# Hybrid decoder trunk: the ends of both attentions and the norms behind them issued in another order and on other engines

## Chip, cores and metric

One core of one Trainium2 chip runs the whole program. The metric is the device time of one execution in microseconds (us), less is better. Before the change three runs gave a median of 1220.93 us (1218.38 to 1221.46).

The core has five engines that run side by side and wait for each other by semaphores: TensorE (PE in the profile; PEld is its weight load), VectorE (DVE), ScalarE (ACT), GpSimd (POOL) and SyncE (SP), which here issues nearly all DMAs.

## The reference

A trunk of two layers over 512 positions of 1024 values. Layer 0 mixes with two groups of attention heads (MoBA and NSA), layer 1 with forgetting attention (FoX); behind each mixer stands an MLP with squared ReLU, and a norm stands ahead of each of the four.

```python
def reference(x, rel_bias, mix_norm, mlp_norm, even_w_in, even_w_out, ...):
    h = x
    for layer in range(DEPTH):
        hn = rmsnorm(h, mix_norm[layer])
        i = layer // 2
        if layer % 2 == 0:
            h = h + moba_nsa_mixer(hn, even_w_in[i], even_w_out[i], rel_bias, ...)
        else:
            h = h + fox_mixer(hn, odd_w_in[i], odd_b_forget[i], odd_w_out[i])
        h = h + sqrelu_mlp(rmsnorm(h, mlp_norm[layer]), mlp_w1[layer], mlp_w2[layer])
    return rmsnorm(h, final_norm)
```

Both mixers end in `o @ w_out`, where `o` holds 16 heads of 64 columns. The kernel treats them as 8 pairs of heads, so `w_out` falls into 8 blocks of 128 rows, one for each pair. `sqrelu_mlp` is `relu(h @ w1)**2 @ w2` with 4096 inner columns.

## The kernel before

**Data.** The 512 positions are four tiles `x0` to `x3` of 128 x 1024 float32 in SBUF (in the rows of the trace all are `x`), the residual stream `h`. Each product in float32 is made of three passes: both factors are split into a high part (rounded, by ScalarE) and a low part (the rest, by a subtraction), and `mm3` (L136 to L138) multiplies high by high, high by low and low by high into one PSUM bank. Its matmuls write up to 128 x 512.

**Weights.** `split` (L94, L101) takes a loaded block of 128 x 1024 from the pool `raw` (5 buffers), lets ScalarE write the high part (L94) and VectorE or GpSimd the low part (L101) into a buffer of the pool `whl` (3 buffers). Which of the two makes the low part is read from a string of D and P (`MIX0_LOW`, `FOX_LOW`), letter by letter.

**Order.** Each mixer runs a list of steps, `MIX0_ORDER` and `FOX_ORDER`. In it `k`/`n`/`m` (layer 0) and `k`/`p` (layer 1) are logits, softmax and products with V for a pair of heads; `x` loads the first four blocks of `w1` and squares them on ScalarE (L429, each leaves a sum); `y` multiplies these sums on TensorE (L411), makes a power-of-two scale from them on VectorE (L416 to L419), and splits the four blocks by that scale into float16 parts (L438 on ScalarE, L439 on VectorE); `o67:01` is the output projection of the pairs 6 and 7 for the tiles 0 and 1. The framework's scheduler then orders each engine's instructions by priority; head work has a higher one (`prio`), so that independent matmuls fill in between. Behind that each engine works through its own queue in order.

**Output projection.** `out_proj` makes for each tile two groups of matmuls (3 for each pair of heads) in two PSUM banks named `acc`, and after each group VectorE adds the bank to the tile (L673, 128 x 512). The bank is free for the next group but one when that add is done. Before, layer 0 splits the last four pairs' products in groups of 1, 6 and 23, layer 1 in groups of 2 pairs.

**Softmax of layer 0.** Logits (L509) are read by VectorE with the bias and the row's minimum (L513), turned by ScalarE's exponential (L514), normalised by GpSimd (L516), transposed on TensorE (L531), copied to a high part by ScalarE (L533, `PTh`) and to a low part by VectorE (L534, `PTl`), and multiplied with V (L604). A pair's result is put together by ScalarE (L645) and VectorE (L646) and split by GpSimd (L498 high, L654 low) into `O`.

**Softmax of layer 1.** Logits (L548) of Q and K, which ScalarE copies from PSUM (L1461, L1464) and VectorE and GpSimd split (L492, L494, L498); VectorE L552, ScalarE L553; high and low parts `HL` by ScalarE (L563, L570), VectorE (L571) and GpSimd (L564); a DMA transposes them into `HT` (L573), and TensorE multiplies by V (L627).

**The norm ahead of the MLP.** `norm_t16`, for each tile: ScalarE squares the tile and sums it (L377); three small operations of VectorE make a power-of-two factor from the sum's bits (L380 to L382); VectorE multiplies tile, factor and gain in two halves (L384); TensorE transposes (L389, 8 for a tile); ScalarE and VectorE copy high and low parts out (L392, L393). The gain row `g` comes by a DMA (L158). The first MLP stage then multiplies float16 parts in matmuls of 128 x 256, first for the tiles 0 and 1, then for 2 and 3.

Of the kernel before, what the change touches and what calls it, by code (L numbers as in the profile page):

```python
# [49 lines left out]

class Trunk:
# [370 lines left out]
    def up_load(self, layer, s, pool, tag, tiles, squares, behind=None):  # L422
        w = self.I["mlp_w1"][layer]
        raws = [pool.tile([P, W_RAW], F32, tag=tag, name=self.nm("w1")) for _ in range(4)]
        for f, raw in enumerate(raws):
            c = 512 * s + P * f
            self.nc.sync.dma_start(raw.rearrange("p (k c) -> p k c", k=KD), w[:, c:c + P].rearrange("(k p) c -> p k c", p=P))
            with self.tc.issue_after(behind.ins) if behind else ExitStack():
                self.nc.scalar.activation(tiles[f][:, 1], raw, AF.Square, accum_out=squares[:, f:f + 1])  # L429
# [19 lines left out]
    def prepare_mlp(self, layer):  # L449
# [9 lines left out]
        def rest():
            self.scales16(st[:, 0], st[:, 1:], "s", self.pv_last)(self.v_last)  # L460
            self.first_up = self.up_split(raws, st[:, 1:], tiles), st[:, 1:]
        self.prepare_rest = rest
# [74 lines left out]
    def softmax_t(self, passes, band):  # L537
# [6 lines left out]
        for qi in (3, 2, 1, 0):  # L544
            w = P * (qi + 1)
            ps = self.psum("s" if qi % 2 else "pt")
            for i, (q, k) in enumerate(passes):
                nc.tensor.matmul(ps[:, :w], q[:, qi * P:(qi + 1) * P], k[:, :w],  # L548
# [108 lines left out]
    def out_proj(self, w, arg, os, hs, pools={}):  # L657
# [3 lines left out]
        if tiles[0] == 0:  # L661
            for i in pairs:
                self.wout[i] = self.rows(w, P * i, 1, pools.get(i))[0]
# [890 lines left out]
```

## Time and profile before

| | |
|---|---|
| median of three runs | 1220.93 us |
| the profiled execution | 1220.05 us |
| its span in the trace | 1218.0 us |
| mean granted TensorE clock | 0.993 |

The span is what the trace shows from the first to the last instruction; the 2.05 us around it are not in the trace. A row of the timeline has start, length, engine, line, operation, tile written and tiles read, shapes, and in brackets the idle time of the engine ahead of the row and what ended it. In a row of the windows each engine has its busy time in the stretch and in brackets its instructions, then come the granted clock (1.00 is full), the DMA engines' share and their GB/s. Matmuls overlap in their records: the step between the starts of two is what one costs.

### The profile page before, as it was taken

To read this page: it belongs to the slowest core of one execution; us is meant where nothing else is said; L and a number is where in the kernel's file an instruction comes from. 1 tells how busy PE (TensorE), PEld (TensorE's weight loads), DVE (VectorE), ACT (ScalarE), POOL (GpSimd) and SP (SyncE) were. 2 spreads that over 40 slices of the span, in tenths; PEclk is the share of its full clock that TensorE was granted. 3 is DMA by queue.
4 is the path that set the end of the run, shared out by engine and by line. 5 is a ranking of instruction groups with operands and counts; after the bars stand their busy time and mean duration, and the time that the engine had idled before them with its cause. 6 is when DMAs were issued, how large, how long until landed. Compare 5 with 4: busy or idle time off the path is not lost. (4 is left out here: it accounts for less than half of the span.)

```text
span 1218.0 us, 17306 instructions
## 1 busy us (share of the span) xinstructions
PE 1181.6 (97%) x6203; PEld 872.3 (72%) x6203; DVE 934.0 (77%) x1741; ACT 738.9 (61%) x1355; POOL 344.8 (28%) x391
## 2 busy tenths in 40 slices
PE   9999999998999999999998999999999999999997
PEld 7789987876855665666687878887675566656666
DVE  6877678888779687978767677676859787779865
ACT  7447656684686575656416785685478466746442
POOL 3434557451030322111001553443003032112104
PEclk9999999999999999999999999999999999999999
DMA  8962332114333244224005475545734413442201
GB/s 238 335 179 59 87 104 79 53 44 139 90 112 115 83 138 139 68 72 149 1 27 143 115 160 119 130 112 120 212 105 121 139 45 111 138 121 64 75 1 70
DMA packets 183729, 134.28 MB, mean 110 GB/s; under 512 B 48163, under 2 KB 158923, under 8 KB 183644
## 3 DMA queue, kind: packets, MB, share of 16 engines
q1 hardware_dynamic: 183484, 132.95, 38.8%
q8 instruction: 49, 0.80, 0.3%
q14 instruction: 36, 0.29, 0.1%
q10 hardware_dynamic: 160, 0.23, 0.1%
HBM read 120.28 MB, written 7.64 MB: 105 GB/s over the span
## 5 line engine op out<-in xcount | busy, mean ns | idle before, releaser
L136 PE MATMUL acc<-x,w 128*128 128x512 f16 (+1 forms) x512 | 187.6, 366 | 0.0
L138 PE MATMUL acc<-x,w 128*128 128x512 f16 (+1 forms) x512 | 187.4, 366 | 0.0
L137 PE MATMUL acc<-x,w 128*128 128x512 f16 (+1 forms) x512 | 187.3, 366 | 0.0
L1300 PE MATMUL s<-whl,sp 128*128 128x512 f32 x672 | 180.2, 408 | 0.1
L1300 PEld LDWEIGHTS s<-whl,sp 128*128 128x128 f32 x672 | 126.1, 188 | 32.5 <-DVE x L1309 1.4
L1253 DVE TENSOR_TENSOR whl<-w,whl 128x1024 fp32r<-128x1024 f32 x98 | 122.1, 1261 | 13.8 <-ACT whl L1252 13.8
L1252 ACT ACTIVATE whl<-w 128x1024 fp32r<-128x1024 f32 x98 | 99.8, 1048 | 53.4 <-DVE w L1258 34.4
L1309 DVE SCALAR_TENSOR_TENSOR x<-s,nr,x 128x512 f32<-128x512 f32 x112 | 82.2, 744 | 62.6 <-PE s L1300 62.6
L94 ACT ACTIVATE whl<-raw 128x1024 fp32r<-128x1024 f32 (+1 forms) x75 | 77.7, 1044 | 49.2 <-PE acc L138 20.2
L1219 POOL TENSOR_TENSOR t<-act 128x512 f32<-128x512 f32 x14 | 25.6, 1831 | 282.5 <-ACT act L1198 171.6
L136 PEld LDWEIGHTS <-w 128*128 128x128 f16 x576 | 57.1, 99 | 56.9 <-issue 10.9
L138 PEld LDWEIGHTS <-w 128*128 128x128 f16 x576 | 56.3, 98 | 56.2 <-issue 5.3
L1196 ACT ACTIVATE r<-acc,upsc 128x512 f32<-128x512 f32 x56 | 38.2, 682 | 96.1 <-PE acc L138 96.1
L136 PE MATMUL acc<-xhi,whl 128*128 128x512 f32 x240 | 94.9, 396 | 1.4 <-DVE Q L494 0.9
L138 PE MATMUL acc<-xhi,whl 128*128 128x512 f32 x240 | 94.6, 394 | 1.3 <-POOL whl L101 0.8
L137 PE MATMUL acc<-xlo,whl 128*128 128x512 f32 x240 | 93.9, 391 | 0.0
L137 PEld LDWEIGHTS <-w 128*128 128x128 f16 x576 | 56.5, 98 | 49.4 <-issue 2.4
L1300 PE MATMUL o<-whl,sp 128*128 128x512 f32 x336 | 83.5, 393 | 3.1 <-ACT sp L1208 3.1
L1258 DVE TENSOR_TENSOR w<-w,w 128x1024 f32<-128x1024 f32 x56 | 72.8, 1300 | 10.4 <-DMA w<-in_mlp_w 9.9
L101 DVE TENSOR_TENSOR whl<-raw,whl 128x1024 fp32r<-128x1024 f32 (+2 forms) x54 | 68.9, 1282 | 15.4 <-ACT whl L94 15.2
L439 DVE SCALAR_TENSOR_TENSOR w<-w,upsc,w 128x1024 f16<-128x1024 f32 x56 | 70.6, 1314 | 8.8 <-ACT w L438 8.8
L1300 PEld LDWEIGHTS o<-whl,sp 128*128 128x128 f32 x336 | 62.9, 188 | 17.4 <-ACT sp L1208 3.9
(339 smaller groups left out, 2923.4 us busy)
## 6 DMA issues: line engine op xcount, KB each, us to landing
w<-in_mlp_w SPq DMA_DIRECT2D x120, 512.0 KB
raw<-in_odd_w_in SPq DMA_DIRECT2D x22, 512.0 KB
raw<-in_even_w_in SPq DMA_DIRECT2D x20, 512.0 KB
band<-bias_dram SPq DMA_DIRECT2D x24, 256.0 KB
bias_dram<-bias_rows SPq DMA_DIRECT2D x16, 320.0 KB
raw<-in_even_w_out SPq DMA_DIRECT2D x8, 512.0 KB
raw<-in_mlp_w SPq DMA_DIRECT2D x8, 512.0 KB
raw<-in_odd_w_out SPq DMA_DIRECT2D x8, 512.0 KB
```

The source lines that it names most:

```text
L94: nc.scalar.activation(hl[:, 0, :n], raw[:, :n], AF.Copy)
L101: eng.tensor_tensor(hl[:, 1, :n], raw[:, :n], hl[:, 0, :n].bitcast(F32), op=ALU.subtract)
L136: mm(ps, ahl[0], bhl[0], start=first, stop=False)
L137: mm(ps, ahl[0], bhl[1], start=False, stop=False)
L138: self.mm_last = mm(ps, ahl[1], bhl[0], start=False, stop=last)
L439: nc.vector.scalar_tensor_tensor(t[:, 1], raw, y, t[:, 0], op0=ALU.mult, op1=ALU.subtract)
L1196: nc.scalar.activation(r, ps, AF.Relu, scale=undo[:, 1, f:f + 1])
L1252: nc.scalar.activation(t[:, 0], src, AF.Copy)
L1253: nc.vector.tensor_tensor(t[:, 1], src, t[:, 0].bitcast(F32), op=ALU.subtract)
L1258: nc.vector.tensor_tensor(out, a_, b_, op=op)
L1300: mm = lambda l, r, first, last: nc.tensor.matmul(ps, l, r, start=first, stop=last, skip_group_check=True)
L1309: self.added = nc.vector.scalar_tensor_tensor(hv, ps, by_token(t), hv, op0=ALU.mult, op1=ALU.add)
```

## The change

- **Order lists.** Layer 0: `x` moves ahead of the pair `m2`, `y` ahead of `m3`, the last pair. Before, the projection of the pairs 1 and 7 stood behind `m3` together with 6, 2 and 3; now 17 keeps its groups for the tiles 0 to 3, pair 6 alone remains for the tiles 2 and 3, and 6, 2, 3 go together for the tiles 0 and 1. So 12 adds follow in place of 16. A new step `z` splits the `w1` blocks two at a time. Layer 1: 45 runs for all four tiles ahead of 67.
- **Late output weights.** The rows for the pairs 2 and 3 (layer 0) and 5, 6, 7 (layer 1) are loaded into buffers of the softmax's pool `pP`, where the probabilities of done heads stood (`out_row`); their low part is made by the engine named there.
- **Squares.** In layer 0 they are issued behind the last product with V known then (`behind`); in layer 1 they are written to a buffer of its own, and not to the `w1` buffers.
- **Scale.** In layer 1 its matmul is issued behind the first of the last pair's logits.
- **Norm.** Tile times gain on GpSimd, the small factor on GpSimd in two operations, and the multiplication by it on ScalarE.

```diff
-MIX0_ORDER = "... n3 k3 m2 x0 m3 y o17:0123 o6:012 o23:01 o6:3 o23:23"
+MIX0_ORDER = "... n3 k3 x0 m2 y m3 o17:0123 o6:23 z01 o623:01 z23 o23:23"
-FOX_ORDER = "... o23:0123 x1 p7 y o45:012 o67:01 o45:3 o67:23"
+FOX_ORDER = "... o23:0123 x1 p7 y o45:0123 z01 o67:01 z23 o67:23"
...
-                nc.scalar.activation(xn[:, c], hs[t][:, c], AF.Square, accum_out=ssq[:, t + i:t + i + 1])
+                nc.scalar.activation(scratch[:, c], hs[t][:, c], AF.Square, accum_out=ssq[:, t + i:t + i + 1])
...
-            v.tensor_scalar(one(near).bitcast(I32), one(ssq).bitcast(I32), 1, None, op0=ALU.logical_shift_right)
-            v.tensor_scalar(one(near).bitcast(I32), one(near).bitcast(I32), -1, ROOT_BITS, op0=ALU.mult, op1=ALU.add)
-            v.tensor_tensor(one(scale), one(near), gain, op=ALU.mult)
-            for c in halves:
-                v.scalar_tensor_tensor(xn[:, c], hs[t][:, c], one(scale), g[:, c], op0=ALU.mult, op1=ALU.mult)
+            nc.gpsimd.tensor_tensor(xn, hs[t], g, op=ALU.mult)
+            nc.gpsimd.tensor_scalar(one(near).bitcast(I32), one(ssq).bitcast(I32), -0.5, ROOT_BITS, op0=ALU.mult, op1=ALU.add)
+            nc.gpsimd.tensor_tensor(one(scale), one(near), gain, op=ALU.mult)
+            nc.scalar.activation(xn, xn, AF.Copy, scale=one(scale))
...
+    def out_row(self, w, i, raw, parts, eng):
+        nc = self.nc
+        raw = raw.tile([P, PTW if raw is self.pP else W_RAW], F32, tag="P" if raw is self.pP else "raw", name=self.nm("raw"))
+        nc.sync.dma_start(raw[:, :D], w[P * i:P * i + P, :])
+        t = parts.tile([P, 2, W_RAW], FR, tag="whl", name=self.nm("whl"))
+        hl = t[:, 0], t[:, 1]
+        nc.scalar.activation(hl[0], raw[:, :D], AF.Copy)
+        eng.tensor_tensor(hl[1], raw[:, :D], hl[0].bitcast(F32), op=ALU.subtract)
+        return hl
...
+            how = {2: (self.pP, self.whl, nc.vector), 3: (self.pP, self.whl, nc.gpsimd)}
...
-                    self.prepare_mlp(int(arg))
+                    self.prepare_mlp(int(arg), self.pv_last)
...
-                    self.prepare_rest()
-                    self.phase = "D"
+                    self.prepare_rest(self.pv_last, self.v_last)
+                elif op == "z":
+                    for f in arg:
+                        self.prepare_part(int(f))
...
+            how = {5: (self.pP, last, nc.vector), 6: (self.pP, self.whl, nc.gpsimd), 7: (self.pP, self.whl, nc.gpsimd)}
...
-                    self.prepare_mlp(int(arg))
+                    self.prepare_mlp(int(arg), None, last.tile([P, 2, W_RAW], FR, tag="whl", name="dump2")[:, 0])
...
-                    self.prepare_rest()
-                    self.phase = "D"
+                    self.prepare_rest(self.logits_mid, self.v_mid)
```

In the rows below a name's number is its buffer, and each row is one instruction of the engine's queue in order. The first place is TensorE at the products with V of layer 0's last head (`o_3347` before, `o_3353` now). Before:

```order
L604 MATMUL o_3347<-PTl_3327,vm_104 128x384
L604 MATMUL o_3347<-PTh_3326,vm_106 128x128
L604 MATMUL o_3347<-PTl_3327,vm_106 128x128
L136 MATMUL acc_3454<-whl_3451,O_2624 128x512
L137 MATMUL acc_3454<-whl_3451,O_2624 128x512
L138 MATMUL acc_3454<-whl_3451,O_2624 128x512
L136 MATMUL acc_3459<-whl_3451,O_2624 128x512
L137 MATMUL acc_3459<-whl_3451,O_2624 128x512
L138 MATMUL acc_3459<-whl_3451,O_2624 128x512
L604 MATMUL o_3347<-PTh_3326,vm_105 128x256
```

Now, up to the first matmul that needs this head's own result (`O_3364`):

```order
L605 MATMUL o_3353<-PTh_3332,vm_103 128x512
L532 MATMUL pt_3348<-ident,P_3302 128x128 x2
L605 MATMUL o_3353<-PTl_3333,vm_103 128x512
L605 MATMUL o_3353<-PTh_3332,vm_104 128x384
L605 MATMUL o_3353<-PTl_3333,vm_104 128x384
L605 MATMUL o_3353<-PTh_3332,vm_106 128x128
L605 MATMUL o_3353<-PTl_3333,vm_106 128x128
L605 MATMUL o_3353<-PTh_3332,vm_105 128x256
L605 MATMUL o_3353<-PTl_3333,vm_105 128x256
L136 MATMUL acc_3480<-whl_3477,O_3364 128x512
```

The matmuls of the output projection that stood between and behind the last head's products (pair 6 with `O_2624` and others) now stand ahead of them.

The second place is VectorE a little earlier, where the last two heads' softmax runs now. Now:

```order
L437 SCALAR_TENSOR_TENSOR w_474_3083<-w_475_3084,upst_3080,w_474_3083 128x1024
L437 SCALAR_TENSOR_TENSOR w_474_3083<-w_476_3085,upst_3080,w_474_3083 128x1024
L688 TENSOR_TENSOR x_126<-acc_3425,x_126 128x512
L437 SCALAR_TENSOR_TENSOR w_474_3083<-w_477_3086,upst_3080,w_474_3083 128x1024
L688 TENSOR_TENSOR x_126<-acc_3426,x_126 128x512
L514 ISA P_3238,sst_3239<-s_3261,band_3236 128x512
L514 ISA sst_3239 128x1
L514 ISA P_3302,sst_3303<-s_3304,band_3300 128x128
L514 ISA sst_3303 128x1
L437 SCALAR_TENSOR_TENSOR w_474_3083<-w_478_3087,upst_3080,w_474_3083 128x1024
```

Before, the same four blocks (there L439) came on VectorE behind the last head:

```order
L673 TENSOR_TENSOR x_124<-acc_3479,x_124 128x512
L439 SCALAR_TENSOR_TENSOR w_502_3215<-w_503_3216,upst_3212,w_502_3215 128x1024
L439 SCALAR_TENSOR_TENSOR w_502_3215<-w_504_3217,upst_3212,w_502_3215 128x1024
L439 SCALAR_TENSOR_TENSOR w_502_3215<-w_505_3218,upst_3212,w_502_3215 128x1024
L673 TENSOR_TENSOR x_107<-acc_3494,x_107 128x512
L439 SCALAR_TENSOR_TENSOR w_502_3215<-w_506_3219,upst_3212,w_502_3215 128x1024
```

So the splits moved from behind the softmax of the last pair into it.

The third place is ScalarE in layer 1, at the copies of K and Q for the last pair. Before:

```order
L1461 ACTIVATE Q_1206_8259<-acc_8192 64x512
L429 ACTIVATE w_1242_8454,upst_8451<-w_1243_8455 128x1024
L429 ACTIVATE w_1242_8454,upst_8451<-w_1244_8456 128x1024
L1464 ACTIVATE K_1204_8249<-acc_8222 64x512
L429 ACTIVATE w_1242_8454,upst_8451<-w_1245_8457 128x1024
L429 ACTIVATE w_1242_8454,upst_8451<-w_1246_8458 128x1024
L94 ACTIVATE whl_8590<-raw_8588 128x1024
L1464 ACTIVATE K_1208_8261<-acc_8222 64x512
```

Now:

```order
L427 ACTIVATE dump_8440,upst_8441<-w_1242_8447 128x1024
L1481 ACTIVATE Q_1199_8236<-acc_8181 64x512
L94 ACTIVATE whl_8373<-raw_8371 128x1024
L1481 ACTIVATE Q_1203_8248<-acc_8181 64x512
L427 ACTIVATE dump_8440,upst_8441<-w_1243_8448 128x1024
L1484 ACTIVATE K_1201_8238<-acc_8211 64x512
L94 ACTIVATE whl_8572<-raw_8570 128x1024
L1484 ACTIVATE K_1205_8250<-acc_8211 64x512
```

The four squares moved ahead of the copies of K (two of them far ahead).

More of the change, by code (lines that the diff above doesn't have):

```diff
@@ L420, in scales16, with up_load @@
         return step
-    def up_load(self, layer, s, pool, tag, tiles, squares, behind=None):
+    def up_load(self, layer, s, pool, tag, tiles, squares, behind=None, scratch=None):
         w = self.I["mlp_w1"][layer]
@@ L447, in up_tiles, with prepare_mlp @@
         return [t[:, j] for j in range(4)]
-    def prepare_mlp(self, layer):
+    def prepare_mlp(self, layer, behind=None, scratch=None):
         nc = self.nc
@@ L455, in prepare_mlp, with rest, part @@
         tiles = self.up_tiles(0)
-        raws = self.up_load(layer, 0, self.raw, "raw", tiles, st[:, 0])
+        raws = self.up_load(layer, 0, self.raw, "raw", tiles, st[:, 0], behind, scratch)
         nc.scalar.activation(g8, g8, AF.Square, accum_out=st[:, 0, 4:5])
[L459 to L462, printed above, removed]
+        self.first_up = [], st[:, 1:]
+        def rest(product, after):
+            self.scales16(st[:, 0], st[:, 1:], "s", product)(after)
+        def part(f):
+            self.first_up[0].extend(self.up_split(raws[f:f + 1], st[:, 1:, f:f + 1], tiles[f:f + 1]))
+        self.prepare_rest, self.prepare_part = rest, part
     def norm_t(self, hs, g, plain=False):
@@ L547, in softmax_t @@
             for i, (q, k) in enumerate(passes):
-                nc.tensor.matmul(ps[:, :w], q[:, qi * P:(qi + 1) * P], k[:, :w],
-                                 start=i == 0, stop=i == len(passes) - 1)
+                self.logits_last = nc.tensor.matmul(ps[:, :w], q[:, qi * P:(qi + 1) * P], k[:, :w],
+                                                    start=i == 0, stop=i == len(passes) - 1)
             seg = pt[:, SEG[qi]:SEG[qi] + w]
@@ L655, in split_o, with out_proj @@
         return hl
[L657 removed]
+    def out_row(self, w, i, raw, parts, eng):
[7 more added lines that the diff above has]
+        return hl
+    def out_proj(self, w, arg, os, hs, how={}):
         nc = self.nc
         pairs, tiles = ([int(a) for a in part] for part in arg.split(":"))
[L661 to L663 removed]
+        for i in pairs:
+            if i not in self.wout:
+                self.wout[i] = self.out_row(w, i, *how[i]) if i in how else self.rows(w, P * i, 1)[0]
         for t in tiles:
[L665 to L671 removed]
+            ps = [self.psum("acc") for _ in range(2)]
+            for part in (pairs[:-1], pairs[-1:]) if len(pairs) > 2 and t == tiles[0] else (pairs,):
+                for n in range(2):
+                    for i in part:
+                        o, wc = os[i], self.wout[i]
+                        self.mm3(ps[n], (o[:, 0, t * P:(t + 1) * P], o[:, 1, t * P:(t + 1) * P]),
+                                 (wc[0][:, n * 512:(n + 1) * 512], wc[1][:, n * 512:(n + 1) * 512]),
+                                 i == pairs[0], i == pairs[-1])
+            for n in range(2):
                 hv = hs[t][:, n * 512:(n + 1) * 512]
[L673 removed]
+                nc.vector.tensor_tensor(hv, ps[n], hv, op=ALU.add)
     def band_setup(self, pool):
@@ L1164, in mlp @@
             self.bcast_row(g, I["mlp_norm"][layer])
-            x, short = self.norm_t16(hs, g, gain[:, 0], mg)
+            scratch = ma.tile([P, 2, 2, S // 2], F32, tag="act", name=self.nm("act"))
+            x, short = self.norm_t16(hs, g, gain[:, 0], mg, scratch.rearrange("p a b c -> p (a b c)"))
             after = self.x_act, self.x_dve
```

30 lines of the change are left out of this document (14 added, 16 removed).

## Prediction

> **What bounds the kernel now.** I read the page's busy times first, then windows of 20 us, then the waits, and last the timeline of the two stretches that the windows point at.
>
> ```profile
> PE 1181.6 (97%) x6203; PEld 872.3 (72%) x6203; DVE 934.0 (77%) x1741; ACT 738.9 (61%) x1355; POOL 344.8 (28%) x391
> ```
>
> TensorE is busy for 97% of the span: only the 36 us in which it is idle, and the time in which it runs slowly, can be won. The change adds and removes no matmul.
>
> ```profile
> 240.00:260.00 20.00, 17.75 (x93) 14.25 (x91) 15.16 (x49) 17.44 (x46) 10.79 (x17) 0.91 0.16 53
> 280.00:300.00 20.00, 16.73 (x72) 11.97 (x70) 18.19 (x26) 9.15 (x11) 3.81 (x4) 0.91 0.63 181
> 840.00:860.00 20.00, 18.43 (x103) 13.37 (x104) 17.04 (x38) 13.36 (x29) 4.06 (x8) 0.91 0.58 137
> 860.00:880.00 20.00, 18.02 (x86) 14.29 (x85) 16.50 (x29) 5.80 (x10) 0.00 (x0) 1.00 0.76 219
> ...
> PE acc L136 <- DVE x L673: 7.0, 8, 1.9
> ```
>
> The first rows are windows, the last one of the waits. At the ends of both attentions TensorE is idle for 2 to 3 us of 20, VectorE is the fullest engine beside it, and the bracket's releaser is the add of a group to its tile: 7.0 us in 8 waits. These are the stretches that the change rewrites. I price each by one moment, the **first float16 matmul** of the MLP, behind which nothing that TensorE waits for is changed.
>
> **Layer 0 now.**
>
> ```profile
> 261.23 0.45 PE L604 MATMUL o<-PTh,vn 128*128 128x512 f32 x1
> ...
> 288.00 0.39 PE L137 MATMUL acc<-whl,O 128*128 128x512 f32 x1
> 288.23 0.40 PE L138 MATMUL acc<-whl,O 128*128 128x512 f32 x1
> 288.86 0.50 PE L136 MATMUL acc<-whl,O 128*128 128x512 f32 x1 [0.23 <-DVE x L673]
> ...
> 290.50 0.50 PE L136 MATMUL acc<-whl,O 128*128 128x512 f32 x1 [0.68 <-DVE x L673]
> ...
> 292.73 0.63 PE L137 MATMUL acc<-whl,O 128*128 128x512 f32 x1
> 293.16 0.63 PE L138 MATMUL acc<-whl,O 128*128 128x512 f32 x1
> ...
> 309.43 1.03 PE L389 MATMUL pt<-ident,xn 128*128 128x128 f32 x8
> 311.70 0.28 PE L136 MATMUL acc<-x,w 128*128 128x256 f16 x1
> ```
>
> Reader, see two prices. A matmul of 128 x 512 costs 0.23 us, the step from 288.00 to 288.23; narrower ones I take at their share of columns, and a transpose at 0.1. And after short waits the step grows to 0.43 (292.73 to 293.16): the window's clock falls to 0.91, and a dip of that kind costs about 1.8 us (9% of 20). [...]
>
> From 261.23, where the fourth NSA product with V begins in both orders, TensorE in the new order does three heads' products (15 units of 512 columns, 3.5 us), 22 transposes (2.2) and 18 matmuls of the projection (4.2). With 2 us of waits between, an estimate from what the windows on either side lose, it comes to the last pair's logits at **273.2**. From there to the float16 stage it has 96 matmuls of the projection (22.4), logits and products with V of two heads (20 units, 4.7) and 36 transposes (3.6): 30.7, so 303.9 without any wait. The waits, from the queue orders of both files and these rows:
>
> ```profile
> 294.62 3.66 DVE L439 SCALAR_TENSOR_TENSOR w<-w,upst,w 128x1024 f16<-128x1024 f32 x3
> ...
> L673 DVE TENSOR_TENSOR x<-acc,x 128x512 f32<-128x512 f32 x72 | 48.6, 683 | 13.2 <-PE acc L138 12.8
> L101 DVE TENSOR_TENSOR whl<-raw,whl 128x1024 fp32r<-128x1024 f32 x51 | 66.2, 1304 | 15.0 <-ACT whl L94 14.9
> L513 DVE CUSTOM_DVE_ANT_0 P<-s,band 128x512 f32<-128x512 f32 x24 | 16.4, 682 | 3.6 <-PE s L509 3.5
> L515 DVE RECIPROCAL sst<-sst 128x1 f32<-128x1 f32 x96 | 14.0, 154 | 7.2 <-ACT P L514 6.6
> L498 POOL TENSOR_SCALAR O<-o 128x512 fp32r<-128x512 f32 x8 | 5.0, 619 | 16.6 <-DVE x L673 10.5 <-DVE o L646 6.0
> L645 ACT ACTIVATE o<-o 64x512 f32<-64x512 f32 x16 | 9.5, 594 | 2.8 <-PE o L604 1.9 <-POOL O L654 0.5
> L101 POOL TENSOR_TENSOR whl<-raw,whl 128x1024 fp32r<-128x1024 f32 x21 | 51.9, 2471 | 44.5 <-ACT whl L94 44.1 <-DMA K<-fox_rows 0.3
> ```
>
> - *VectorE's block, 5.1 us.* Between the last pair's logits VectorE now has four splits (4 x 3.66 / 3 = 4.9), six adds (about 0.62 each, back to back), one low part of weights (1.30), five passes over logits (two at 0.68, three narrower by their columns, 2.4) and six reciprocals (0.9): 13.2 us without a gap. TensorE behind them has 24 matmuls, half the logits and 9 transposes, 7.5 us, and four of its groups wait for one of these adds (0.75, 1.1, 0.2, 1.75 us as I lay the rows out), a transpose for its probabilities 1.35. Before, the splits stood behind the softmax and made TensorE wait there; that wait goes, this one comes.
> - *The last head without filling, 3.0 us.* Exponential, copy, low part, transpose, product follow each other with nothing between; before, matmuls of the projection lay between. Two new things stand in this chain: ScalarE's copy of pair 3's weights is ahead of the last exponential (1.05), and its low part on GpSimd (2.47) ahead of the last normalisation.
> - *Pair 3's result, 2.6 us.* Last product, copy (0.59), add (0.68), rounding (0.62) and then TensorE; its low part later by another 0.35. Before, groups of pair 6 covered that.
> - *First tile's norm, 1.9 us.* The tile's add (TensorE's next group waits 0.75 for it), the product on GpSimd beside ScalarE's square, the small factor, the factor's multiplication on ScalarE (as L438 below, 1.07); 18 matmuls (4.2) cover all but 0.75 of that, and the copies of tile 1 leave 0.4. The trace has no such product: its nearest rows are GpSimd's subtraction, 2.47 for 128 x 1024, and 1.28 for half of it (below), so 2.5. Nor has it an operation on 128 x 1 on GpSimd: nothing and 0.62 (128 x 512) are the ends, I take 0.25; the other ends move each wait by 0.5 to 0.7.
>
> Together 12.6, so 316.5, and with one dip 318.3, against 311.70: +4.8 or +6.6. I take **+6** (-1 to +8: the first two waits may nest, and VectorE's block may drain early).
>
> **Loads and covers in layer 0.**
>
> ```profile
> 286.70 0.33 SPq L90 DMA_DIRECT2D raw<-in_even_w_out  x1
> 287.48 0.33 SPq L158 DMA_DIRECT2D g<-in_mlp_norm  x1
> ...
> 290.11 1.06 ACT L94 ACTIVATE whl<-raw 128x1024 fp32r<-128x1024 f32 x1 [2.03 <-DMA raw<-in_even_w_out]
> ```
>
> A row block lands 3.4 us behind its issue (286.70 to 290.11), and ScalarE was idle for 2.03 of them. Pair 3's block takes the buffer of pair 2's, so its load is issued only when VectorE has made pair 2's low part, which stands at the end of the block above: it lands some 3.4 us later, just as ScalarE wants it. A later landing would add up to 3 us. The gain row `g`, issued at 287.48, now stands on SP behind the last product with V (about 299.6), and the next weights behind it: it lands at 303, 2 us ahead of tile 0, and the weights are needed only in the float16 stage; I count nothing, and if that cover is gone it costs what is late. The low parts of pairs 1 and 6 go from VectorE to GpSimd, ahead of normalisations near 250, where GpSimd is busy for 10.79 of 20 us: nothing, up to 0.5 if they meet. Squares of layer 0 keep their place: nothing.
>
> **Layer 1 now.**
>
> ```profile
> 831.80 1.06 ACT L429 ACTIVATE w<-w 128x1024 f16<-128x1024 f32 x1 [3.05 <-PE acc L137]
> 837.66 0.60 ACT L1464 ACTIVATE K<-acc 64x512 fp32r<-64x512 f32 x1
> ...
> 831.83 0.39 PE L136 MATMUL acc<-whl,O 128*128 128x512 f32 x1
> 834.15 0.51 PE L136 MATMUL acc<-whl,O 128*128 128x512 f32 x1 [0.78 <-DVE x L673]
> 839.00 0.50 PE L548 MATMUL s<-K,Q 128*128 128x512 f32 x1 [0.53 <-POOL K L498]
> 840.80 0.50 PE L548 MATMUL s<-K,Q 68*128 68x512 f32 x1 [0.93 <-DVE K L492]
> 847.37 1.82 PE L627 MATMUL o<-HT,v 128*64 128x512 f16 x24
> ```
>
> ScalarE waits 3.05 us to begin the four squares (their output goes to a buffer that TensorE still reads) and is then in them, with K's first copy between and a weight copy behind, so that K's second copy comes only at 837.66: that is behind two of TensorE's waits (0.53, 0.93). With a buffer of their own the squares run in that idle time and K is copied from 832. TensorE then has 36 matmuls and the logits of two heads, 8.4 + 2.3 = 10.7 us, from 831.83: products with V at 843.1 with 0.6 of waits left, **4.3 us sooner** than 847.37.
>
> ```profile
> 853.28 4.26 ACT L438 ACTIVATE w<-w,upst 128x1024 f16<-128x1024 f32 x4
> 850.47 1.34 POOL L564 TENSOR_TENSOR HL<-P,HL 128x128 f16<-128x128 f32 x2 [0.85 <-ACT HL L563]
> 856.75 1.79 PE L627 MATMUL o<-HT,v 128*64 128x512 f16 x23 [0.53 <-DMA HT<-HL]
> 863.41 0.50 PE L136 MATMUL acc<-whl,O 128*128 128x512 f32 x1 [1.90 <-DVE x L673]
> 880.89 0.39 PE L136 MATMUL s<-x,w 128*128 128x256 f16 x2
> ```
>
> Most is given back. ScalarE's four splits (4.26) now stand ahead of the last two copies of the last head's probabilities: by the queue they run from 846.3 to 850.6, the copies take 0.6 and GpSimd's low parts end at about 852.3, against 851.81 before (850.47 + 1.34); transposed by a DMA it reaches TensorE 4.9 us later (851.81 to 856.75), at 857.2, and TensorE, early, waits 2.0 there. Ahead of that VectorE's low part, splits and adds (the same block as in layer 0, 4 x 1.22 among it) make it wait 3.3 (1.35, 0.3, 1.65). The 1.90 at 863.41 goes. At the end stands the norm: GpSimd's 2.5 for tile 2 is queued ahead of tile 1's small factor, so tile 1's transposes wait 1.45. Products with V end at 859.2, then 78 matmuls of the projection (18.2), transposes 1.6, that wait and 0.4 for the copies: float16 matmuls at 880.8 with all projection done, against 880.89 plus one group (1.4) before: -1.5. I take **-1**, for a dip (1.8) may come or not (-5 to +2).
>
> The norm's product may be weighed by the page GPSIMD Engine Reference of the Trainium skill: its section 4.1, Engine selection, puts elementwise products on VectorE, since GpSimd takes about twice as long with two inputs. The rows agree (2471 against 1304 ns). By that rule the product had better stay, and the waits of 1.45 and 0.75 for the norm would not come: 1223.
>
> **Sum.** 1220.05 + 6 - 1 = **1225 us**; the profiled run lies 0.9 under the median of 1220.93, which I leave in the range. About 0.3% (3.7 us) is what a measurement can tell from no change.
>
> **Rivals.**
> - *Faster.* VectorE's block does not bind in layer 0: if ScalarE gives it the split's high parts a little later, the adds slip ahead of them. It decides where the adds wait less than 0.2 us each; then 5.1 and the dip go, layer 0 comes to -1, and layer 1 keeps the 4.3 as far as the DMA allows (-4): 1215. For it speaks that VectorE loses four adds (2.7), eight half products and smalls; against it that the order lists the splits first. Chance 0.17.
> - *A wash.* Layer 0 loses 3 (block and tail partly nested), layer 1 wins 3: 1220. Chance 0.24; it is also what comes if the change does little of what it says: layer 0's squares stay in their place in ScalarE's queue.
> - *GpSimd binds.*
>
> ```profile
> 284.86 1.82 DVE L101 TENSOR_TENSOR whl<-raw,whl 128x1024 fp32r<-128x1024 f32 x1
> 284.31 1.28 POOL L654 TENSOR_TENSOR O<-o,O 128x512 fp32r<-128x512 f32 x1
> ```
>
> While GpSimd subtracts, VectorE's subtraction takes 1.82 in place of 1.30. Eight products, four low parts and more add some 28 us of such time; if each costs VectorE 0.5 us where TensorE waits for it, and the norm waits twice: 1230. Chance 0.12. The page GPSIMD Engine Reference of the Trainium skill, section 1, Specifications, has the two engines share their SBUF interfaces; these two rows agree.
> - *Forecast*, 1225: chance 0.47, of which 0.07 lies under 1224.6 and so within 0.3%.
>
> Faster 0.17, within 0.3% 0.24 + 0.07 = 0.31, slower 0.40 + 0.12 = 0.52. The range 1216 to 1231 leaves out the far half of the first rival (0.09) and of the third (0.06).
>
> **What would show it.** Right: a first float16 matmul near 318 in place of 311.70 and, counted from the start of the FoX projection, 1 us sooner in layer 1; waits of L136 for the add (L688) at 280 to 290; TensorE idle some 2 us behind the last product with V, released by GpSimd's L499. ScalarE's squares ahead of 832 in layer 1, and K's waits gone. Wrong: adds that wait less than 1 us in all in layer 0, a landing of pair 3's block that ends a longer wait, or tile 1's transposes on time.

## The result, and the profile after

The changed kernel takes **1237.65 us** (median of four runs, 1236.8 to 1238.69) against 1220.74 for the kernel before beside it: ratio **1.0139** (95% interval 1.0123 to 1.0155), 1.4% slower. The profiled execution took 1236.8 us, its span is 1234.7 and its mean granted clock 0.991, against 1218.0 and 0.993.

The page's busy times of the kernel after:

```profile
PE 1183.5 (96%) x6203; PEld 874.2 (71%) x6203; DVE 910.8 (74%) x1691; ACT 747.5 (61%) x1363; POOL 372.4 (30%) x421
```

Its windows of 20 us, with the columns as before:

```profile
280.00:300.00 20.00, 14.50 (x73) 10.37 (x71) 15.17 (x34) 10.63 (x24) 10.00 (x10) 1.00 0.10 27
300.00:320.00 20.00, 16.73 (x77) 12.64 (x78) 8.96 (x13) 10.21 (x18) 11.96 (x12) 0.91 0.80 213
820.00:840.00 20.00, 19.59 (x131) 17.64 (x132) 12.96 (x35) 14.12 (x39) 9.69 (x12) 0.91 0.60 129
860.00:880.00 20.00, 15.49 (x75) 11.23 (x74) 15.04 (x18) 8.85 (x12) 9.58 (x6) 0.91 0.64 162
```

VectorE has lost 23 us of work and GpSimd gained 28, as the change says. TensorE has the same 6203 matmuls, and in the windows at both ends of attention it is now idle for 3.3 to 5.5 us of 20 (0.4 in 820 to 840), where before it was 1.6 to 3.3. VectorE, the fullest engine of that stretch before, is busy for 15.17 us of 280 to 300 in place of 18.19, and the stretch became longer all the same. TensorE's waits for the adds are 5.4 us in all over the span, against 7.0; what is new are other waits, shown below.

I split the 16.7 us by which the span grew at two landmarks, the float16 matmul and the first Q projection of FoX. From the timeline of TensorE before, with the last logits of layer 0 that are spoken of below:

```profile
268.64 0.40 PE L509 MATMUL s<-KL,QS 128*128 128x512 f32 x1
...
660.79 0.48 PE L136 MATMUL acc<-xhi,whl 128*128 128x512 f32 x1
```

and after:

```profile
318.47 0.38 PE L136 MATMUL acc<-x,w 128*128 128x256 f16 x2 [0.25 <-ACT x L390]
668.67 0.48 PE L136 MATMUL acc<-xhi,whl 128*128 128x512 f32 x1
898.11 0.38 PE L136 MATMUL acc<-x,w 128*128 128x256 f16 x2 [1.04 <-ACT x L390]
```

Layer 0's attention gives +6.8 (318.47 - 311.70), its MLP +1.1 (to +7.9 at 668.67 - 660.79), layer 1's attention **+9.3** (from 668.67 to 898.11 is 229.4; before, from 660.79 to 880.89, 220.1), and the rest, up to the last matmul, -0.6.

**Layer 0 after**, the timeline of TensorE from the last pair's logits on:

```profile
273.79 0.28 PE L409 MATMUL s<-upst,ones 128*128 128x5 f32 x2
273.93 0.31 PE L510 MATMUL s<-KS,QS 128*128 128x128 f32 x1
281.79 0.50 PE L136 MATMUL acc<-whl,O 128*128 128x512 f32 x1 [0.45 <-DVE x L688]
283.58 0.50 PE L136 MATMUL acc<-whl,O 128*128 128x512 f32 x1 [0.83 <-DVE x L688]
286.25 0.44 PE L532 MATMUL pt<-ident,P 128*128 128x128 f32 x2 [1.11 <-POOL P L517]
288.37 0.40 PE L510 MATMUL s<-KL,QS 128*128 128x512 f32 x1
289.65 0.50 PE L136 MATMUL acc<-whl,O 128*128 128x512 f32 x1 [0.88 <-DVE x L688]
297.88 0.50 PE L605 MATMUL o<-PTh,vm 128*128 128x512 f32 x1 [1.04 <-ACT PTh L534]
302.47 0.80 PE L136 MATMUL acc<-whl,O 128*128 128x512 f32 x1 [2.11 <-POOL O L499]
```

The scale's two small matmuls (L409) stand just ahead of the last pair's logits and write into a bank of `s`, which those logits use too. The last logits start at 288.37 (before at 268.64), so the last pair's softmax runs with less and less of the projection left to cover it.

**Layer 1 after**, first ScalarE:

```profile
812.96 1.06 ACT L427 ACTIVATE dump<-w 128x1024 fp32r<-128x1024 f32 x1 [0.87 <-DMA w<-in_mlp_w]
839.92 1.06 ACT L427 ACTIVATE dump<-w 128x1024 fp32r<-128x1024 f32 x1 [4.22 <-DMA w<-in_mlp_w]
845.79 1.06 ACT L427 ACTIVATE dump<-w 128x1024 fp32r<-128x1024 f32 x1 [2.66 <-DMA w<-in_mlp_w]
846.97 0.59 ACT L1484 ACTIVATE K<-acc 64x512 fp32r<-64x512 f32 x1
848.74 0.59 ACT L1484 ACTIVATE K<-acc 64x512 fp32r<-64x512 f32 x1
860.61 4.25 ACT L436 ACTIVATE w<-w,upst 128x1024 f16<-128x1024 f32 x4
864.77 0.60 ACT L564 ACTIVATE HL<-P 128x128 f16<-128x128 f32 x2
```

TensorE:

```profile
820.40 0.36 PE L136 MATMUL acc<-whl,xhi 128*128 128x256 f32 x1 [1.75 <-DVE K L493]
848.38 0.50 PE L549 MATMUL s<-K,Q 128*128 128x512 f32 x1 [2.05 <-POOL K L499]
858.26 1.82 PE L628 MATMUL o<-HT,v 128*64 128x512 f16 x24
872.55 3.21 PE L628 MATMUL o<-HT,v 128*64 128x512 f16 x23 [3.14 <-DMA HT<-HL]
```

GpSimd, and SyncE's queue of DMAs:

```profile
865.15 2.48 POOL L565 TENSOR_TENSOR HL<-P,HL 128x128 f16<-128x128 f32 x2 [3.68 <-ACT HL L564]
...
835.84 4.30 SPq L574 DMA_TRANSPOSE HT<-HL  x1
840.23 0.53 SPq L425 DMA_DIRECT2D w<-in_mlp_w  x1
```

The squares no longer wait for TensorE. They wait for their own loads: the last one's load (L425) is issued at 840.23, behind a DMA transpose that holds SyncE's queue for 4.30 us, and its square starts at 845.79. K's copies are queued behind the squares, so they start at 846.97 and 848.74; before it was 834.02 and 837.66. 7.9 us of that distance came with what stands ahead of FoX. Counted from the first Q projection of FoX, the copies are 5.1 and 3.2 us later than before, and the products with V behind them (858.26, before 847.37) 3.0 us later, not earlier.

### The profile page after: what moved, and what is told of

Read it like the earlier page. It is cut to its first block, busy times and chain, and to the rows that moved or that the text cites. A ratio compares the mean times of both kernels' runs of the same rounds, so it can differ in the third digit from the quotient of the medians.

```text
span 1234.7 us, 17284 instructions
## 1 busy us (share of the span) xinstructions
PE 1183.5 (96%) x6203; PEld 874.2 (71%) x6203; DVE 910.8 (74%) x1691; ACT 747.5 (61%) x1363; POOL 372.4 (30%) x421
## 5 line engine op out<-in xcount | busy, mean ns | idle before, releaser
L94 ACT ACTIVATE whl<-raw 128x1024 fp32r<-128x1024 f32 (+1 forms) x70 | 72.2, 1043 | 40.1 <-PE acc L138 18.2
L101 POOL TENSOR_TENSOR whl<-raw,whl 128x1024 fp32r<-128x1024 f32 x24 | 59.0, 2459 | 51.2 <-ACT whl L94 50.5
L1277 DVE TENSOR_TENSOR w<-w,w 128x1024 f32<-128x1024 f32 x56 | 69.0, 1231 | 5.2 <-DMA w<-in_mlp_w 4.8
```

The costliest lines, as they stand in the source:

```text
L94: nc.scalar.activation(hl[:, 0, :n], raw[:, :n], AF.Copy)
L101: eng.tensor_tensor(hl[:, 1, :n], raw[:, :n], hl[:, 0, :n].bitcast(F32), op=ALU.subtract)
L1277: nc.vector.tensor_tensor(out, a_, b_, op=op)
```

## The experiments

"To FoX", "FoX" and "rest" are the profiled execution's differences to before, in us: up to the first Q projection of FoX, from there to layer 1's first float16 matmul, and from there to the last matmul. They are one execution each and hold the clock's ups and downs; the ratio is what was timed. Rows that keep layer 1 (or 0) "old" have it as before the change.

| kernel | to FoX | FoX | rest | clock | median us (runs) | ratio [95%] |
|---|---|---|---|---|---|---|
| after | +7.9 | +9.3 | -0.6 | .991 | 1237.65 (4) | 1.0139 [1.0123, 1.0155] |
| e1 layer 0 alone | +6.4 | -0.3 | -0.7 | .995 | 1226.99 (4) | 1.0071 [1.0048, 1.0094] |
| e2 layer 1 alone | +0.6 | +9.9 | -0.8 | .988 | 1227.55 (4) | 1.0075 [1.0058, 1.0091] |
| e3 squares to `w1` tiles | +9.0 | +6.7 | -0.4 | .991 | 1236.42 (4) | 1.0149 [1.0124, 1.0174] |
| e4 both norms old | +9.8 | +6.9 | -1.2 | .990 | 1234.74 (4) | 1.0128 [1.0111, 1.0145] |
| e5 layer 1's scale late | +7.8 | +5.1 | +0.7 | .990 | 1234.71 (4) | 1.0114 [1.0070, 1.0157] |
| e6 before + squares' buffer | -0.6 | +5.8 | -0.8 | .990 | 1222.85 (10) | 1.0029 [1.0007, 1.0050] |
| e7 e6, loads earlier | -0.2 | +9.0 | 0.0 | .989 | 1228.89 (6) | 1.0071 [1.0045, 1.0097] |
| e8 layer 0's scale late | +0.5 | +9.7 | -1.2 | .993 | 1232.87 (4) | 1.0093 [1.0057, 1.0130] |
| e9 both scales late | +1.2 | +5.3 | +0.4 | .991 | 1224.30 (5) | 1.0043 [1.0027, 1.0059] |
| e10 e9 + e3 | +1.5 | +5.5 | -1.4 | .993 | 1225.41 (7) | 1.0040 [1.0023, 1.0056] |
| e11 e1, scale late | -0.2 | +0.4 | +0.1 | .994 | 1220.30 (12) | 1.0005 [0.9995, 1.0015] |
| e12 e11, norm old | -0.3 | +1.1 | -1.0 | .993 | 1219.88 (12) | 1.0003 [0.9989, 1.0017] |
| e13 e10, layer 1's norm old | +0.7 | +3.4 | -1.5 | .993 | 1221.95 (10) | 1.0024 [1.0008, 1.0041] |
| e14 e13, order 1 old | +1.1 | +3.5 | -0.9 | .992 | 1222.34 (10) | 1.0030 [1.0016, 1.0045] |
| e15 e12, adds and splits apart | -1.5 | -0.2 | -0.1 | .994 | 1218.50 (12) | 1.0002 [0.9987, 1.0017] |
| e16 scale's bank `acc` | +3.6 | +11.8 | +1.2 | .986 | 1235.72 (4) | 1.0130 [1.0108, 1.0152] |
| e17 scale's bank `o` | +1.1 | +11.3 | +1.2 | .990 | 1233.11 (4) | 1.0120 [1.0099, 1.0140] |

**e1 and e2: one layer each.**

```diff
 e1 (fox)
-            how = {5: (self.pP, last, nc.vector), 6: (self.pP, self.whl, nc.gpsimd), 7: (self.pP, self.whl, nc.gpsimd)}
+            how = {7: last}
...
-                    self.prepare_mlp(int(arg), None, last.tile([P, 2, W_RAW], FR, tag="whl", name="dump2")[:, 0])
+                    self.prepare_mlp(int(arg))
...
 e2
-MIX0_ORDER = "... n3 k3 x0 m2 y m3 o17:0123 o6:23 z01 o623:01 z23 o23:23"
+MIX0_ORDER = "... n3 k3 m2 x0 m3 y o17:0123 o6:012 o23:01 o6:3 o23:23"
-            how = {2: (self.pP, self.whl, nc.vector), 3: (self.pP, self.whl, nc.gpsimd)}
+            how = {}
```

In both, the other layer also has the order, the scale's place and the norm of before.

> The change in layer 0 alone (order, late weights, squares behind the last product with V, norm on GpSimd there); layer 1 as before. Theory A, that the two layers add up and that layer 0 costs what its stretch shows: first float16 matmul of layer 0 at 318.5, 6.8 us over before, the FoX stretch as before, 1227.5 us. Rival B, that layer 0's new end shifts something that layer 1 pays for (loads, clock): over 1230 us with waits of K's copies near 820 also here.

> The change in layer 1 alone; layer 0 as before. Theory A: all of the loss behind 640 us belongs to layer 1's own edits, so 1220.7 + 9 to 10 = 1230 us, with TensorE's wait for K's low part (1.75) and for K's rounding (2.05) both there. Rival B: 1224 us or less, since part of it came with layer 0.

Each layer costs about half, 0.7% and 0.75%, and together they make the 1.4%. So layer 1 is not the small gain that was forecast.

**e3, e4, e5: one part taken out of the whole change.**

```diff
 e3
-                    self.prepare_mlp(int(arg), None, last.tile([P, 2, W_RAW], FR, tag="whl", name="dump2")[:, 0])
+                    self.prepare_mlp(int(arg))
 e4
-            x, short = self.norm_t16(hs, g, gain[:, 0], mg, scratch.rearrange("p a b c -> p (a b c)"))
+            x, short = self.norm_t16_old(hs, g, gain[:, 0], mg, None)
 e5 (fox)
-                    self.prepare_rest(self.logits_mid, self.v_mid)
+                    self.prepare_rest(self.pv_last, self.v_last)
```

> The changed kernel with one thing undone: the squares of layer 1 write to the weights' own tiles again, which TensorE still reads, so they start later. Theory A (squares that stand early in ScalarE's queue wait there for their loads, and the softmax and K's copies wait behind them): the stretch from 805 to 834 gets its 2.6 us back and K's copies are late as before, so 1235 us, the wait of 1.75 at 820 gone. Rival C (the waits come from the low part of late weights that stands on GpSimd ahead of K's rounding): the waits stay, 1238 us or more.

> The changed kernel with the norm's products on VectorE again, in both layers. Theory A: the norm's own waits go, 1.26 and 1.04 us in layer 1 and 0.4 and 0.25 in layer 0, so 1234.7 us. Rival D (GpSimd's products also slow VectorE down beside them): 1231 us or less. Rival E (VectorE is then late with its adds and splits, as it is the fuller engine): 1237 us or more.

> The changed kernel with the scale of layer 1's first weights taken, as before, behind the products with V of pair 6 and the last low part, so that the four splits stand behind the last head's copies on ScalarE. Theory A (the splits' 4.25 us ahead of these copies make the last transpose by DMA late): the wait of 3.14 us for it falls under 1, and the time to 1235 us. Rival F (the transpose is late because GpSimd's low parts take 2.48 in place of 1.3 us beside VectorE): the wait stays over 2 us, 1237 us.

None of the three gives back more than a quarter of a per cent, and none is clearly off 1.0139 by its interval. In e3 TensorE's waits for K of 1.75 and 2.05 us are gone (one of 0.84 has come) and the products with V start 1.1 us sooner than before, counted from FoX. But behind them it waits 5.5 us for adds (1.4 in after), once 3.44, so little of that is left at the end. In e5 TensorE's wait for the transposed probabilities falls from 3.14 to

```profile
868.21 1.79 PE L628 MATMUL o<-HT,v 128*64 128x512 f16 x23 [0.99 <-DMA HT<-HL]
```

0.99 us: the four splits of 4.25 us no longer stand ahead of the last head's copies (864.77 above). That and the FoX column (4.2 less than in after) point to the scale; its timed gain is unclear here, and e9 shows it better.

**e6 and e7: the squares' buffer alone, and its loads earlier.**

```diff
 e6 (before)
-                    self.prepare_mlp(int(arg))
+                    self.prepare_mlp(int(arg), None, last.tile([P, 2, W_RAW], FR, tag="whl", name="dump2")[:, 0])
 e7 (e6)
-FOX_ORDER = "... p6 o23:0123 x1 p7 y ..."
+FOX_ORDER = "... x1 p6 o23:0123 p7 y ..."
```

> The kernel before with one part of the change: the squares of layer 1 have a buffer of their own. The step of the prediction (they run while ScalarE is idle, and K is copied earlier): 4.3 us sooner, 1216.5 us. Theory A (they stand in ScalarE's queue and wait there for loads that come no sooner than before; softmax and K's copies wait behind): 3 to 4 us lost between 805 and 834, nothing won behind it, 1223 to 1225 us.

> As the run with the squares' own buffer alone, but with the loads asked for one pair earlier, ahead of the softmax of pair 6 and of the weights of pairs 2 and 3. Theory A (it is the landing of the loads that counts): no wait for these loads near 820 to 846, K copied early, the waits of 0.53 and 0.93 us of before gone: 1217 to 1220 us. Rival G (the weights of pairs 2 and 3, loaded later for it, come late): a new wait for them, 1222 us or more.

The step that was to win 4.3 us makes the kernel before 0.3% slower (0.07 to 0.5). One of ScalarE's waits in e6, at the end of layer 1's attention (what waits, what for: us in all, times, longest), then the last loads of the squares in SyncE's queue and TensorE's products with V:

```profile
ACT dump L468 <- DMA w<-in_mlp_w: 8.0, 3, 5.8
...
825.71 5.84 SPq L615 DMA_TRANSPOSE HT<-HL  x1
831.65 0.53 SPq L466 DMA_DIRECT2D w<-in_mlp_w  x1
...
850.16 1.82 PE L669 MATMUL o<-HT,v 128*64 128x512 f16 x24
```

The last two of these loads in the queue of before:

```profile
825.31 1.91 SPq L427 DMA_DIRECT2D w<-in_mlp_w  x2
```

and in e7 a row of TensorE:

```profile
838.80 0.79 PE L136 MATMUL acc<-whl,O 128*128 128x512 f32 x1 [3.11 <-ACT whl L94]
```

In e6 the squares wait 8.0 us for their loads, and the last load even comes later than before: it now stands behind a DMA transpose of the softmax, at 831.65, where before both left from 825.31 on, behind all three transposes. The products with V start at 850.16, 3.4 us later than before counted from FoX. Loading a pair earlier (e7) moves the lateness to the projection's weights, which share the `raw` buffers and the queue: ScalarE waits for those 12.4 us in three waits, TensorE 3.11 behind it, and e7 is the slower of the two.

**e8, e9, e10: the scales late.**

```diff
 e8
-MIX0_ORDER = "... n3 k3 x0 m2 y m3 o17:0123 o6:23 z01 o623:01 z23 o23:23"
+MIX0_ORDER = "... n3 k3 x0 m2 m3 y o17:0123 o6:23 z01 o623:01 z23 o23:23"
```

e9 is this with e5's edit, e10 with e3's as well.

> The changed kernel with the scale of layer 0's first weights taken, as before, behind the last pair, so that the four splits leave VectorE's block between the last logits. The step of the prediction (the block makes TensorE wait 5.1 us): waits for adds near 280 to 290 fall under 1 us in all, and the splits come back in ScalarE's and VectorE's queue behind the softmax; first float16 matmul at 315 to 316, 1235 us. Rival: the splits are as late there as they were before, 318.5, 1237.5 us.

> The changed kernel with both scales late, as in the two runs that took them late one by one. Theory H (the early splits of both layers are most of the loss, and the two do not overlap): 8.8 us come back by layer 0's first float16 matmul and 3.8 by the end of layer 1, of which the first gives 1 to 2 back in the MLP behind it: 1226 to 1228 us. Rival I (one of the two was luck with the clock's dips): 1231 us or more.

> As the run with both scales late, and the squares of layer 1 write to the weights' tiles again, so that what is left of the change is the order of the late weights, their places and engines, and the norm. Theory H: the 3.7 us between 805 and 834 come back too, with no new wait behind, since nothing waits early for the scale now: 1222 to 1224 us. Rival: the wait for the last transpose grows, as it did when the squares alone were undone (12 us between the two last products with V), 1230 us or more.

TensorE in e8:

```profile
267.06 0.40 PE L510 MATMUL s<-KL,QS 128*128 128x512 f32 x1
...
296.04 0.50 PE L136 MATMUL acc<-whl,O 128*128 128x512 f32 x1 [2.62 <-DVE x L688]
309.65 0.38 PE L136 MATMUL acc<-x,w 128*128 128x256 f16 x2 [0.25 <-ACT x L390]
```

The last logits start at 267.06 and not 288.37; the waits for the adds are now longer (2.62 and 1.27, both behind splits), and still the float16 stage starts at 309.65, 8.8 us ahead of after and 2.05 ahead of before. The lead over before isn't kept: at FoX e8 is 0.5 behind before. With layer 1's scale late too (e9 against e8) FoX falls by 4.4 and the ratio from 1.0093 to 1.0043 (the intervals just touch). With late scales the squares' buffer is worth nothing either way (e9 and e10 agree).

**e11 and e12: layer 0 alone, scale late; then with the old norm. e13 and e14: e10 with layer 1's old norm; then with its old order.**

```diff
 e11 (e1): as e8
 e12 (e11), e13 (e10): norm_t16_old in layer 0, in layer 1
 e14 (e13)
-FOX_ORDER = "... p7 y o45:0123 z01 o67:01 z23 o67:23"
+FOX_ORDER = "... p7 y z0123 o45:012 o67:01 o45:3 o67:23"
```

> Layer 1 wholly as before; in layer 0 the change without its early scale: late weights in places of done probabilities, the new order of the projection, low parts on GpSimd, norm on GpSimd and ScalarE. Theory H: the run with layer 0 alone less the 7.4 us that the late scale gave up to FoX: 1219 to 1220 us, no difference from before that can be measured. Rival J (these edits win what the early scale hid, 2 us at the first float16 matmul): 1217 us or less.

> As the run before it, with the norm of layer 0 on VectorE as before too. If the norm on GpSimd costs what I counted (1.9 us for the first tile, part of it there before): 1 us less, 1218 to 1219. If it relieves VectorE behind the late splits: 1 to 2 us more, 1221.

> As the run with both scales late and the squares in the weights' tiles, with layer 1's norm on VectorE as before; left in layer 1 are the order, the places and the engines of the late weights. Theory K (the norm's waits of 1.27, 1.04 and 0.25 us are half of what layer 1 still loses): 1223 us. Rival L (VectorE is the later engine there, and the weights' order is all of the loss): 1225.5 us or more.

> As the run before it, with layer 1's projection in its old order (pairs 4 and 5 for three tiles, then 6 and 7 for two, then the rest), the late weights still loaded into places of probabilities and their low parts on GpSimd. Theory M (the order costs: four tiles of pairs 4 and 5 ahead leave less to fill with behind the last product): 1220.5 us. Rival N (the low parts on GpSimd and the places cost): as the run before it.

e1 and e11 differ only in the scale's place: 1.0071 against 1.0005. All the rest of layer 0's change (order of the projection, places of the weights, GpSimd's low parts, the norm) costs nothing that can be measured, and the norm there is worth nothing (e12). In layer 1 the old norm brings 5.5 to 3.4 us and 1.0040 to 1.0024 (the intervals overlap); the order brings nothing (e14). What e14 keeps of layer 1's change, the places and the low parts' engine of the late weights, still shows 1.0030, which no run takes apart.

**e15: adds and splits apart.** The waits of e8 (2.62 and 1.27) stand behind splits, so e15 lets an add go between them:

```diff
 e15 (e12)
-MIX0_ORDER = "... m2 m3 y o17:0123 o6:23 z01 o623:01 z23 o23:23"
+MIX0_ORDER = "... m2 m3 y o17:0123 o6:23 o623:0 z01 o623:1 z23 o23:23"
...
-            self.first_up[0].extend(self.up_split(...))
+            with self.tc.issue_after(after.ins) if after else ExitStack():
+              self.first_up[0].extend(self.up_split(...))
```

> As the run with layer 0's late scale and the norm on VectorE, layer 1 as before; the first two splits of layer 0 are held behind the first tile's adds and the other two behind the second's. If the adds' wait of 2.63 us behind the first two splits is a true cost: 1217 to 1218 us, faster than before. If the splits are then late for the tiles behind: 1220 us, the wait comes back elsewhere.

TensorE's longest wait for an add in e12's layer 0:

```profile
296.59 0.70 PE L136 MATMUL acc<-whl,O 128*128 128x512 f32 x1 [2.63 <-DVE x L730]
```

and at the same place in e15:

```profile
294.35 0.50 PE L136 MATMUL acc<-whl,O 128*128 128x512 f32 x1 [0.55 <-DVE x L731]
```

The wait falls from 2.63 to 0.55 and the profile is 1.2 us ahead of e12 at FoX, but the ratio is 1.0002 (0.9987 to 1.0017): no version here measurably beats the kernel before.

**e16 and e17: the early scale kept, only its PSUM bank changed.**

```diff
 e16 (after)
-            self.scales16(st[:, 0], st[:, 1:], "s", product)(after)
+            self.scales16(st[:, 0], st[:, 1:], "acc" if layer == 0 else "s", product)(after)
```

e17 has `"o"` in place of `"acc"`.

> The changed kernel with one word changed: in layer 0 the scale's small matmul writes to a bank named acc and not to one of the two banks named s, which the logits use in turn. Scale and splits stay early. Theory P (what costs in layer 0 is that the last pair's logits stand behind the scale's bank, and with them the whole softmax behind the products): the last logits run near 268 in place of 288, first float16 matmul at 310 to 313, 1229 to 1232 us. Theory of the forecast (VectorE's block of splits and adds is what costs): 316 or later, 1235 us or more.

> As the run before it, with the scale in a bank named o, which the products with V use in turn. Theory P: the same, 310 to 313 and 1229 to 1232 us, if the last pair's products do not wait for that bank; if they do, 2 to 3 us more.

TensorE in e16:

```profile
269.28 0.40 PE L510 MATMUL s<-KL,QS 128*128 128x512 f32 x1
272.80 0.28 PE L409 MATMUL acc<-upst,ones 128*128 128x5 f32 x2
312.68 0.38 PE L136 MATMUL acc<-x,w 128*128 128x256 f16 x2 [0.25 <-ACT x L390]
```

and the float16 stage in e17:

```profile
310.58 0.38 PE L136 MATMUL acc<-x,w 128*128 128x256 f16 x2 [0.25 <-ACT x L390]
```

With the bank `acc` the scale still runs at 272.80, but the last logits are at 269.28, ahead of it, and the float16 stage comes at 312.68 in place of 318.47, with `o` at 310.58. So of the 8.8 us between after and e8, 5.8 and 7.9 go with the bank alone; at FoX 4.3 and 6.8 of them are left. That the bank is what keeps the logits back is shown for this stretch.

It is not shown in the time. The ratios 1.0130 and 1.0120 can't be told from after's 1.0139, and 1235.72 us lies where the expectation put the other theory. Behind the landmark of FoX, where nothing was edited, both profiles lose some 4 us against after (2.5 and 2.0 in FoX, 1.8 behind it). Their windows of 20 us there are at a lower granted clock: taken together they lose 10.2 us (e16) and 8.6 us (e17), against 5.4 in after. Whether that comes with the edit or by chance stays open.

## Why the prediction was right or wrong

The direction was right, the size was not: 1225 was forecast with 1231 as the upper end, 1237.65 came. Layer 0 came out near its sum, layer 1 did not.

**Layer 0: the order right, the sum right partly by luck, one cause missed.** +6 was forecast and +6.8 came (+5.1 in e1, which has the same layer 0); the first of the last pair's logits was put at 273.2 and stands at 273.93; the float16 matmul "near 318" stands at 318.47. The terms, from the rows above with three smaller waits of the same chains (0.58, 0.38 and 0.23 in the last head): VectorE's block 3.3 (0.45 + 0.83 + 1.11 + 0.88) for 5.1, the last head 2.2 for 3.0, pair 3's result 2.1 for 2.6, the norm 0.7 (0.43 + 0.25) for 1.9. Each is there and smaller, 8.3 for 12.6 in all. That the sum fits is luck: the work between was reckoned at 30.7 with 1.8 for a dip, and 44.5 us from 273.93 to 318.47 less 8.7 of waits leave 35.9, 3.4 more.

What the forecast didn't see is that most of these waits have one cause. The scale's matmul takes a bank of the logits, the last pair's logits stand behind it, and the softmax with them. TensorE's waits from 258 us to the float16 stage are 10.4 us in after and 3.3 before. With only the bank changed they are 4.7 (e16) and 5.0 (e17). With the scale behind the last pair (e11) they are 3.9: the waits in the last head (but 0.20), that for pair 3's result and the norm's 0.43 are gone, and one wait of 2.63 for an add behind the splits has come.

The moment by which layer 0 was priced, the first float16 matmul, also says less than it seems to. e11 reaches it 2.4 us ahead of before and is 0.2 ahead at FoX, e8 falls from 2.05 ahead to 0.5 behind, e15 keeps 1.5 of 3.4. Why the stretch behind it takes so much back stays open.

**Layer 1: the step that failed** is "With a buffer of their own the squares run in that idle time and K is copied from 832 ... products with V at 843.1 with 0.6 of waits left, 4.3 us sooner than 847.37." It took the wait that the trace named (3.05 us, for a `w1` buffer that TensorE still read) for the only one. Freed of it, the squares stand earlier in ScalarE's queue and wait there for their loads, 7.8 us in three waits in after and 8.0 in e6, and K's copies stand behind them (846.97). One early square (812.96) stands ahead of softmax and copies: in all ten kernels with the buffer TensorE waits 1.75 to 1.82 us for K's low part there (820.40 in after), in those without it that wait is missing. Counted from the first Q projection of FoX, the products with V start 3.0 us later than before in after and 3.4 in e6, where 4.3 sooner was forecast; in e3, with only the buffer taken back, they start 1.1 sooner. By itself the step costs 0.3% (e6) where it was to bring 0.35%; taken back out of the whole change it brings nothing that can be measured (e3, and e10 against e9). Of the 10.3 us between layer 1's forecast (-1) and its profile (+9.3), 7.3 lie ahead of these products and 3.0 behind.

**Layer 1: terms mis-sized.** The wait for the last head's transposed probabilities was forecast at 2.0 and measured 3.14: the splits run ahead of the last copies (860.61 to 864.86), as was read from the queue, but the two low parts on GpSimd (865.15) then took 2.48 us and not 1.34; VectorE runs splits beside them. The early scale, which puts the splits there, was priced at these 2.0 and VectorE's block at 3.3; undoing it (e9 against e8) is worth 4.4 us of FoX and 0.5%. The norm's wait was forecast at 1.45 plus 0.4 and measured 1.26 + 1.04 + 0.27; e13 against e10 puts it at some 2 us in the profile and 0.16% in time, with intervals that overlap.

**Layer 1's sum.** It was -1; the profile gives +9.3. From its rows I reckon K's low part 1.75, the transposed probabilities 2.6 (3.14 - 0.53), the norm 2.6, the add behind them -0.5 (1.36 for 1.90), K's second wait nothing (2.05 for the former 0.53 + 0.93 and 0.78), and four windows at a clock of 0.91 to 0.96 (5.4 us lost) against one at 0.91 before (1.8), 3.6: 10 in all. The last of these is the least certain: it is the granted clock of one execution, and half of it is a dip behind a wait that before has as well, without a dip (last section). Timed, layer 1 alone costs 0.75%, which is 9 us (e2).

**The MLP** was said to be unchanged behind the float16 stage; layer 0's lost 1.1 us in this profile. The waits that are new in its rows are those for low parts of the next norm, 0.27, 0.22 and 0.87 us from 656 to 662. No run tests what they cost.

**The norm on GpSimd.** The rule weighed in the prediction (page GPSIMD Engine Reference of the Trainium skill, section 4.1, Engine selection: two-input products belong on VectorE) agrees with layer 1's profile (e13: FoX +3.4 in place of +5.5) and made no difference in layer 0 (e12).

**The rivals.** "Faster" rested on adds that TensorE waits less than 0.2 us for in layer 0; it waits 0.45, 0.83 and 0.88. "A wash" with layer 1 winning 3 fell with the squares. GpSimd as the bound has a part in the 3.14 and in the norm, but layer 0 with all its GpSimd work and a late scale costs nothing (e11).

## What to carry to other kernels

Before a small operation is moved ahead of a large one, look at which rotating buffer it takes: two matmuls of 5 columns in a bank of the logits put 16 logits matmuls behind them. Moving them, and the splits that hang on them, ahead of the last pair cost 0.7% (e1 against e11). A wait that is removed lets the instruction be queued earlier, where on an in-order engine it may wait longer for something else, with others behind it: follow the instruction's other inputs, loads first, and the queue that issues them. And where several waits are forecast for one stretch, ask first whether they share a cause that one edit would take away.

## What was unexpected of the hardware

**A small operation lasted until the other engine's operation ended.** VectorE's and GpSimd's rows of e8:

```profile
290.20 1.28 DVE L415 TENSOR_SCALAR upst<-upst 128x5 int32<-128x5 int32 x1
291.52 0.17 DVE L416 TENSOR_SCALAR upst<-upst 128x5 int32<-128x5 int32 x1
296.50 4.62 DVE L437 SCALAR_TENSOR_TENSOR w<-w,upst,w 128x1024 f16<-128x1024 f32 x2
...
290.17 1.29 POOL L655 TENSOR_TENSOR O<-o,O 128x512 fp32r<-128x512 f32 x1
...
300.12 1.05 POOL L380 TENSOR_SCALAR nr<-ssq 128x1 int32<-128x1 int32 x1
```

VectorE's operation on 128 x 5 takes 1.28 us and ends at 291.48, with GpSimd's subtraction (291.46); its like takes 0.17 right behind it. GpSimd's operation on 128 x 1 takes 1.05 and ends at 301.17, with VectorE's two splits (301.12); the seven others of its kind in e8 take 0.19. These are two cases, and no run varies them. The forecast's 0.25 lies between.

**The clock dips behind some short waits and not behind others.** TensorE waits at the same place of layer 1 for the same operand, 1.90 us both times. Before:

```profile
710.51 0.39 PE L136 MATMUL acc<-whl,xhi 128*128 128x256 f32 x1 [1.90 <-DVE v L1414]
710.73 0.28 PE L137 MATMUL acc<-whl,xhi 128*128 128x256 f32 x1
710.85 0.28 PE L138 MATMUL acc<-whl,xlo 128*128 128x256 f32 x1
```

and after:

```profile
718.41 0.56 PE L136 MATMUL acc<-whl,xhi 128*128 128x256 f32 x1 [1.90 <-DVE v L1434]
718.77 0.42 PE L137 MATMUL acc<-whl,xhi 128*128 128x256 f32 x1
718.98 0.42 PE L138 MATMUL acc<-whl,xlo 128*128 128x256 f32 x1
```

The step between the last two is 0.12 us before and 0.21 after, where it stays so until 721.76; the granted clock of the windows from 700 to 740 is 1.00 before, 0.96 and 0.95 after. So the length of the wait alone doesn't decide it. Over the kernels of the table the mean clock lies between 0.986 and 0.995, some 11 us of a span of 1230 (an estimate, 0.009 of it). A difference of a few us in one stretch of one profile therefore means little without the timed ratio.
